# Cross-attention output through DRAM: two rounded parts, or one float32 that the reader splits

## The chip, the cores and the metric

The kernel runs on one core of one Trainium2 chip. The metric is the device time of one execution in microseconds (us), the median of several runs. Five engines work side by side, each through its own queue in a fixed order: PE (matrix products; its weight loads are shown as PEld), ACT, DVE and POOL (elementwise work), and SP, which here issues all DMAs.

## The reference

One step of a hybrid encoder layer on 1024 prompt rows and 8 x 16 sample rows, 1152 token rows in all, in float32. After the three token mixers comes a cross-attention with 4 heads of 256 channels into 256 memory rows, then a gated feed-forward network. What matters here:

```python
def cross_attend(u, mk, mv, wq, wo):
    b, n, _ = u.shape
    q = jnp.einsum('bnd,de->bne', u, wq).reshape(b, n, X_HEADS, X_HEAD_DIM)
    s = jnp.einsum('bnhd,bmhd->bhnm', q, mk.astype(q.dtype)).astype(jnp.float32) * (X_HEAD_DIM ** -0.5)
    pr = jax.nn.softmax(s, axis=-1)
    o = jnp.einsum('bhnm,bmhd->bnhd', pr, mv.astype(jnp.float32)).astype(u.dtype)
    return jnp.einsum('bne,ed->bnd', o.reshape(b, n, D_MODEL), wo)
...
    h = h + mix.astype(h.dtype)
    h = h + cross_attend(rmsnorm(h, p['norm_x_g']), mk, mv, p['wq_x'], p['wo_x']).astype(h.dtype)
    h = h + swiglu(rmsnorm(h, p['norm_ffn_g']), p['w_gate'], p['w_up'], p['w_down']).astype(h.dtype)
```

The tensor `o` of this function, 1024 channels by 1152 token rows, is what the change is about.

## The kernel before

**Products in three parts.** PE multiplies in a rounded 32-bit format (float32r). To keep float32 accuracy, each operand x is split into a high part hi (x rounded, a cast on ACT) and a low part lo (x - hi, a subtraction on DVE or POOL), and a product is three matmuls: hi·hi, hi·lo, lo·hi (`mm3`, L337 to L340). In the profile its three matmuls are thus L338, L339 and L340. `split` (L459, work at L462 on ACT and L463 on DVE) makes the two parts.

**Cross-attention, heads 0 to 2.** `x_query` makes the queries of a head. `x_prompt` takes the 1024 prompt rows in four blocks of 256: `scores` (PE, then `x_softmax`, whose exponentials on ACT are L1484, whose row maxima on DVE are L1478) and `values`, which transposes the weights on PE (L1547), splits them (L1550, L1551) and multiplies them with the memory values into the PSUM bank `pso`. `x_sample` treats the 128 sample rows of the head as one block of 128; its loads of cached keys and values are L1575 and L1599, its products L1609. Each block of a head ends in `x_out`. For heads 0 to 2 it splits the 2 x 128 channels of the block into a high and a low tile and stores both into `o_sc` (named `osc` in the profile), a DRAM tensor with eight slabs of 128 channels and two parts for each. For head 3 (L1514 to L1522) it splits straight from PSUM into the resident tiles `direct`; nothing of head 3 goes through DRAM.

**Buffers.** The tiles `pt` come from a pool of four buffers (L75). The exponentials of the prompt rows, the two parts of the transposed weights and the two output tiles of x_out all use it. An output tile is free again when its store has landed.

**Output projection.** `add_rows` (L1316) multiplies slabs 0 to 3 (heads 0 and 1) with the first half of `wo_x` and adds the result to the residual rows `h` (L1332, on DVE, which frees the PSUM bank). It needs the three chunk tiles `first`, each of 384 token rows and four slabs. `finish_rows` does the same with slabs 4 to 7 and the second half: slabs 4 and 5 (head 2) are loaded into the tiles `direct`, slabs 6 and 7 (head 3) are put there by x_out. `load_chunk` (L1390) loads the high and the low part of a chunk with a DMA each. Another loader, `load_unsplit` (L1395), stood already in the kernel for the mixers' output `mix_sc`: it loads plain float32 into the low half of the tile, casts it into the high half (L1400) and subtracts in place (L1401), two slabs at a time.

**Order.** `loads` (L1688) is woven into head 3's steps: two of its steps behind each step of head 3's prompt rows, while `weave` (L1711) mixes `add_rows` with head 3's sample rows. This is the order in which the program states the work; the final order of each engine's queue is set when the kernel is built, by a planner that follows a simulated timeline (`schedule_with_timeline_sim=True`), with priorities raised for some steps (`hp`). At run time each engine goes through its queue in that order.

Of the kernel before, what the change touches and what calls it, by code (L numbers as in the profile page):

```python
# [8 lines left out]
F32 = mybir.dt.float32  # L9
F32R = mybir.dt.float32r  # L10
# [7 lines left out]
P = 128  # L18
# [6 lines left out]
T = SEQ + DEC_B * DEC_S  # L25
NBLK = T // P
CW = 384
# [30 lines left out]
def f32(x):  # L58
    return x.bitcast(F32)
# [3 lines left out]
def tile_hybrid_step(ctx: ExitStack, tc: tile.TileContext, a: dict):  # L63
    nc = tc.nc
    ACT, DVE, POOL, PE, SP = nc.scalar, nc.vector, nc.gpsimd, nc.tensor, nc.sync
# [38 lines left out]
    def pt_t(dt=F32R):  # L104
        return ptp.tile([P, 512], dt, tag="pt", name="pt")
# [40 lines left out]
    for k0 in (0, 2):  # L146
        first_raw.append(st_t(F32))
        SP.dma_start(out=first_raw[-1].rearrange("p (k n) -> p k n", n=512),
                     in_=a["wk_x"][0][k0 * P:(k0 + 2) * P, 0:512].rearrange("(k p) n -> p k n", p=P))
# [81 lines left out]
    def dram(shape, dt, name):  # L231
        return dr.tile(shape, dt, name=name, tag=name)
# [3 lines left out]
    z_sc = dram([T, 512], F32, "zsc")  # L236
    xbc_sc = dram([D, T], F32, "xbcsc")
    mix_sc = dram([8, P, T], F32, "mixsc")
    o_sc = dram([8, 2, P, T], F32R, "osc")
    fc_sc = dram([4, SEQ], F32, "fcsc")  # L240
    fs_sc = dram([4, DEC_B, PAST], F32, "fssc")
    fn_sc = dram([32, DEC_S], F32, "fnsc")
# [109 lines left out]
    def dense_T(w, uc, jobs, homes=(pd,)):  # L352

        n = 0
        units = [(w_unit([(w, c0, P)], 0, KT), f) for c0, f in jobs]
        for c in range(NCH):
            for (wh, wl), consume in units:
                ps = homes[n % len(homes)]()
                n += 1
                uh, ul = uc[c]  # L360
                for k in range(KT):
                    mm3(ps[:, :CW], wh[:, k, :], wl[:, k, :], uh[:, k, :], ul[:, k, :], k == 0, k == KT - 1)
                later = consume(c, ps[:, :CW])
                flush()
                if later:
                    late.append(later)
                yield
# [91 lines left out]
    def split(hi, lo, src, scale=None):  # L459

        if scale is None:
            ACT.copy(hi, src)  # L462
            DVE.tensor_tensor(out=lo, in0=src, in1=f32(hi), op=ALU.subtract)  # L463
        else:
            ACT.activation(hi, src, AF.Copy, scale=scale)
            DVE.scalar_tensor_tensor(lo, src, scale, f32(hi), ALU.mult, ALU.subtract)

    def consume_qk(i, nb, scale, pk=None, sk=None):
        def consume(c, ps):
            hl = [sg_t(F32R)[:, :CW] for _ in range(2)]  # L470
            split(hl[0], hl[1], ps, scale)
            for x in range(2):
                SP.dma_start(out=f32(qk_sc[i, x, :, c * CW:(c + 1) * CW]), in_=f32(hl[x]))
            if pk is not None:
                kt = pt_t(F32)[:, :CW]
                ACT.copy(kt, ps)

                def rows():
                    tp = pT()
                    for j in range(3):  # L480
                        PE.transpose(tp[:, j * P:(j + 1) * P], kt[:, j * P:(j + 1) * P], ident)
                    kn = sg_t()[:, :CW].rearrange("p (j n) -> p j n", j=3)
                    DVE.tensor_copy(kn, tp[:, :CW].rearrange("p (j n) -> p j n", j=3))
                    nj = 3 if c < 2 else 2
                    SP.dma_start(out=pk[c * CW:c * CW + nj * P, nb * P:(nb + 1) * P]
                                 .rearrange("(j p) n -> p j n", p=P), in_=kn[:, 0:nj])
                    if c == 2:
                        SP.dma_start(out=sk[:, nb * P:(nb + 1) * P], in_=kn[:, 2])
                return rows
        return consume  # L490
# [735 lines left out]
    def chunks(cs):  # L1226
        for c in cs:
            yield from norm_in(c)
            if c == 0:
# [8 lines left out]
    first = dense_T(w_in, uc, [(C_SQ, consume_qk(0, 0, QS)), (C_SQ + P, consume_qk(1, 1, QS)),  # L1238
                               (C_SK, consume_qk(2, 0, None, p_k[0], s_k[0]))],
                    (pd, pd, pS, pS))  # L1240
# [145 lines left out]
    def chunk_t(home=None):  # L1386

        return act_t(home=home).rearrange("p (x k t) -> p x k t", x=2, k=4)

    def load_chunk(t, src, c, k0, nk=4):  # L1390
        for x in range(2):
            SP.dma_start(out=f32(t[:, x, 0:nk]),
                         in_=f32(src[k0:k0 + nk, x, :, c * CW:(c + 1) * CW]).rearrange("k p t -> p k t"))

    def load_unsplit(t, src, c, k0):  # L1395

        SP.dma_start(out=f32(t[:, 1]), in_=src[k0:k0 + 4, :, c * CW:(c + 1) * CW].rearrange("k p t -> p k t"))
        for k in (0, 2):
            hi, lo = (t[:, x, k:k + 2] for x in range(2))
            ACT.copy(hi, f32(lo))  # L1400
            DVE.tensor_tensor(out=lo, in0=f32(lo), in1=f32(hi), op=ALU.subtract)  # L1401
# [15 lines left out]
    for c in range(NCH):  # L1417
        load_unsplit(ch[c], mix_sc, c, 4)
# [92 lines left out]
    direct = []  # L1511

    def x_out(hd, po, c0, n):
        if hd == 3:  # L1514

            for db in range(2):
                for c in range(NCH):
                    b0, b1 = max(c0, c * CW), min(c0 + n, (c + 1) * CW)
                    if b0 < b1:
                        hi, lo = (direct[c][:, x, 2 + db, b0 - c * CW:b1 - c * CW] for x in range(2))  # L1520
                        split(hi, lo, po[db][:, b0 - c0:b1 - c0])
            return  # L1522
        hi, lo = pt_t()[:, :2 * n], pt_t()[:, :2 * n]
        for db in range(2):
            split(hi[:, db * n:(db + 1) * n], lo[:, db * n:(db + 1) * n], po[db])
        for x, src in enumerate((hi, lo)):
            SP.dma_start(out=f32(o_sc[2 * hd:2 * hd + 2, x, :, c0:c0 + n]).rearrange("k p t -> p k t"),
                         in_=f32(src).rearrange("p (k t) -> p k t", k=2))

    def x_prompt(hd, q):  # L1530
        qh, ql, _ = q
# [11 lines left out]
        def values(t, pr):  # L1543
            tp = pT()
            for mb in range(2):
                for i in range(2):
                    PE.transpose(tp[:, mb * 256 + i * P:mb * 256 + (i + 1) * P],  # L1547
                                 pr[:, i * 256 + mb * P:i * 256 + (mb + 1) * P], ident)
            ph, pl = pt_t(), pt_t()
            ACT.copy(ph, tp)  # L1550
            DVE.tensor_tensor(out=pl, in0=tp, in1=f32(ph), op=ALU.subtract)  # L1551
            po = [pO() for _ in range(2)]
            for db in range(2):
                for mb in range(2):
                    sl = slice(mb * 256, (mb + 1) * 256)
                    mm3(po[db], vt[:, 0, mb, db * P:(db + 1) * P],
                        vt[:, 1, mb, db * P:(db + 1) * P], ph[:, sl], pl[:, sl], mb == 0, mb == 1)
            x_out(hd, po, t * 256, 256)
# [29 lines left out]
    def x_sample(hd, q, keys=None):  # L1588
# [51 lines left out]
        for db in range(2):  # L1640
            PE.transpose(tp[:, db * P:(db + 1) * P].rearrange("p (e i t) -> p i e t", e=2, t=DEC_S),
                         on[:, db * P:(db + 1) * P], ident)
        x_out(hd, (tp[:, 0:P], tp[:, P:2 * P]), SEQ, P)
        yield

# [30 lines left out]
    def reload_h(n):  # L1676
        for b in range(len(h), n):
            h.append(st_t(F32) if b < 8 else xc_t()[:, :D])
            SP.dma_start(out=h[b], in_=h_sc[b * P:(b + 1) * P, :])
# [5 lines left out]
    first = [chunk_t(act0) for _ in range(NCH)]  # L1685
    direct.extend(chunk_t(act1) for _ in range(NCH))

    def loads():  # L1688
        for c in range(NCH):
            load_chunk(first[c], o_sc, c, 0)  # L1690
            yield
        for c in range(NCH):
            load_chunk(direct[c], o_sc, c, 4, 2)
            yield
        for b in range(4):
            reload_h(b + 1)
            yield

    smp, ld = x_sample(3, q, keys), loads()
    for _ in range(X0):  # L1700
        next(smp, None)
# [425 lines left out]
```

## Time and profile before

| | |
|---|---|
| runs (3) | 1881.21 us median, 1878.07 to 1885.1 |
| profiled execution | 1885.79 us, of it a span of 1884.1 us from first to last instruction |
| mean granted TensorE clock | 0.984 |
| stores to `osc` | 30, from 852.4 to 988.0 us |
| loads from `osc` | 12, from 963.2 to 999.5 us |
| PE waits ended by `act<-osc` | 2.3 and 0.9 us |
| ACT waits of L1484 ended by `osc<-pt` | 22.8 us in 3, the longest 12.2 |

How to read it: times in the views run from the start of the span. A row of a timeline gives start, duration, engine, line and operation, then written and read tiles ("out<-in"), their size and how many rows it merges; a bracket behind it gives the idle time of the engine just before and whose end released it. A row of the windows gives for each engine its busy time and instruction count in that stretch, then the clock that PE was granted (1.00 is full), the mean busy share of the 16 DMA engines and what they moved. Matmuls are pipelined, so a busy PE is not PE at its peak; SPq rows are DMA issues.

### The profile page before, as it was taken

Reading aid. Unit: us, or ns where it says so; the run is one execution under the profiler, and the core shown is the slowest. Engines: PE = TensorE matmul, PEld = TensorE weight load, DVE = VectorE, ACT = ScalarE, POOL = GpSimd, SP = SyncE. Lnnn points to the kernel's source line nnn. Section 1 sums busy time; section 2 is a strip of 40 time slices with the busy share of each in tenths; the row PEclk is TensorE's granted clock in tenths of the full one; section 3 lists DMA queues with packets and bytes.
Section 4 is the critical chain, followed back from the end, with each engine's and each line's share of the span. In section 5 each row is a group of like instructions: output and inputs, shape, how many; then the busy total and the mean of one; then the engine's idle time right before and its main releaser. Section 6 shows DMA issues by size and latency. Waiting matters only on the chain.

```text
span 1884.1 us, 32106 instructions
## 1 busy us (share of the span) xinstructions
PE 1828.7 (97%) x12008; PEld 1631.7 (87%) x12008; DVE 894.1 (47%) x1798; ACT 794.4 (42%) x1703; POOL 619.6 (33%) x921
## 2 busy tenths in 40 slices
PE   7999989999999999999989989999999999999998
PEld 5899878888967767899978889999999999888886
DVE  3412323576656873455534586333333333455554
ACT  6533543545455762343332474333333333344443
POOL 7622424445115673121012107444444542000000
PEclk9999998999989999999999989999999999999999
DMA  9464754437677883257794124333222223657572
GB/s 336 150 187 152 215 143 126 149 107 211 182 217 252 286 291 102 111 134 184 173 327 156 65 76 110 94 87 78 71 71 71 71 71 93 215 185 243 167 250 90
DMA packets 312028, 296.63 MB, mean 157 GB/s; under 512 B 113340, under 2 KB 263844, under 8 KB 311872
## 3 DMA queue, kind: packets, MB, share of 16 engines
q1 hardware_dynamic: 311872, 294.57, 51.4%
q8 instruction: 95, 1.56, 0.3%
q14 instruction: 61, 0.50, 0.1%
HBM read 225.12 MB, written 69.91 MB: 157 GB/s over the span
## 4 chain that ended last, share of the span: by engine, by line
PE 83%; DMA 7%; DVE 4%; POOL 2%; ACT 2%; SPq 1%; issue 1%; DVEq 0%; POOLq 0%; ACTq 0%
PE psd L1920 11%; PE psd L338 10%; PE psd L339 9%; PE psd L340 9%; PE pst L1920 9%; PE pss L1920 4%; PE pss L338 4%; PE pss L340 4%; PE pss L339 4%; PE pso L1920 2%; PE pst L338 2%; PE pst L339 2%; PE pst L340 2%; PE pso L603 1%; DMA act<-acsc 1%
## 5 line engine op out<-in xcount | busy, mean ns | idle before, releaser
L132 POOL TENSOR_TENSOR wl<-wr,wh 128x256 fp32r<-128x256 f32 (+2 forms) x152 | 117.6, 807 | 245.4 <-ACT wh L292 189.7
L338 PE MATMUL psd<-act,wh 128*128 128x384 f32 x528 | 182.1, 345 | 0.0
L340 PE MATMUL psd<-act,wl 128*128 128x384 f32 x528 | 180.6, 343 | 0.0
L339 PE MATMUL psd<-act,wh 128*128 128x384 f32 x528 | 180.2, 342 | 0.0
L1920 PE MATMUL pst<-bT,tr 128*128 128x256 f32 (+1 forms) x1068 | 155.0, 293 | 0.0
L1920 PEld LDWEIGHTS pst<-bT,tr 128*128 128x128 f32 x1068 | 144.9, 188 | 0.1
L340 PE MATMUL psd<-wh,act 128*128 128x512 f32 (+3 forms) x424 | 137.3, 325 | 0.9 <-DMA act<-osc 0.9
L338 PE MATMUL psd<-wh,act 128*128 128x256 f32 (+3 forms) x414 | 133.8, 327 | 2.8 <-DMA act<-osc 2.3
L339 PE MATMUL psd<-wl,act 128*128 128x256 f32 (+3 forms) x414 | 134.9, 326 | 0.9 <-POOL wl L132 0.9
L1920 PE MATMUL psd<-bT,tr 128*128 128x320 f32 (+1 forms) x912 | 133.1, 295 | 0.2 <-POOL tr L132 0.2
L1920 PEld LDWEIGHTS psd<-bT,tr 128*128 128x128 f32 x912 | 125.1, 189 | 0.4 <-POOL tr L132 0.4
L132 POOL TENSOR_TENSOR tr<-u,tr 128x256 fp32r<-128x256 f32 x110 | 82.5, 780 | 101.4 <-ACT tr L1756 83.6
L253 POOL TENSOR_SCALAR sm<-sm 128x1 f32<-128x1 f32 (+2 forms) x27 | 8.8, 327 | 297.7 <-ACT y L2031 207.6
L1895 DVE TENSOR_TENSOR tr<-tr,pst 128x256 f32<-128x256 f32 (+1 forms) x86 | 38.6, 449 | 139.8 <-ACT tr L1892 106.9
L132 POOL TENSOR_TENSOR ws<-ws 128x256 f32<-128x256 f32 (+2 forms) x100 | 71.3, 741 | 97.8 <-DVE ws L532 84.9
L338 PEld LDWEIGHTS psd<-act,wh 128*128 128x128 f32 x528 | 99.4, 188 | 2.7 <-issue 2.0
L340 PEld LDWEIGHTS psd<-act,wl 128*128 128x128 f32 x528 | 99.2, 188 | 2.6 <-issue 2.3
L339 PEld LDWEIGHTS psd<-act,wh 128*128 128x128 f32 x528 | 99.3, 188 | 1.8 <-issue 1.5
L132 POOL TENSOR_TENSOR tr<-raw,tr 128x256 fp32r<-128x256 f32 x94 | 69.4, 768 | 84.2 <-ACT tr L1756 73.0
L338 PEld LDWEIGHTS psd<-wh,act 128*128 128x128 f32 x414 | 79.8, 193 | 11.0 <-DMA act<-osc 2.5
L1756 ACT CAST tr<-u 128x512 fp32r<-128x512 f32 x130 | 76.6, 620 | 28.7 <-PE pst L1920 5.9
L340 PEld LDWEIGHTS psd<-wh,act 128*128 128x128 f32 x424 | 81.5, 192 | 8.2 <-DMA act<-osc 1.4
(645 smaller groups left out, 4663.2 us busy)
## 6 DMA issues: line engine op xcount, KB each, us to landing
u<-w_down SPq DMA_DIRECT2D x40, 512.0 KB
raw<-w_down SPq DMA_DIRECT2D x26, 512.0 KB
st<-qksc SPq DMA_DIRECT2D x48, 256.0 KB
wr<-w_in SPq DMA_DIRECT2D x44, 256.0 KB
tr<-hidsc SPq DMA_DIRECT2D x55, 192.0 KB
hidsc<-tr SPq DMA_DIRECT2D x34, 288.0 KB
qksc<-sg SPq DMA_DIRECT2D x48, 192.0 KB
wr<-cache_sb_k SPq DMA_DIRECT2D x32, 256.0 KB
```

What stands on the lines that cost most here:

```text
L132: POOL.tensor_tensor(out=out[:, a0:a1], in0=in0[:, a0:a1], in1=in1[:, a0:a1], op=op)
L253: POOL.tensor_scalar(v, ss, inv, EPS, ALU.mult, ALU.add)
L338: PE.matmul(out, ah, bh, start=start, stop=False)
L339: PE.matmul(out, ah, bl, start=False, stop=False)
L340: PE.matmul(out, al, bh, start=False, stop=stop)
L603: return PE.matmul(po[r:r + 64, q_], vt[:, 2 * (k0 + i) + j, :], pfs[i][:, sl], start=start and k0 == 0 and (j == 0 or qp > 0), stop=k0 + ...
L1756: ACT.copy(hi, src)
L1895: DVE.tensor_tensor(out=at(out, g), in0=at(x, g), in1=ps[g][:, :GW[g]], op=op)
L1920: PE.matmul(dst[g][:, :GW[g]], x[:, ka], y[:, k, :], start=start and k == 0 and m == 0, stop=stop and k == 3 and m == 2, skip_group_check= ...
```

## The change

`o_sc` holds one float32 per element in place of two parts. `x_out` copies the two channel halves of a block out of PSUM, one on ACT and one on DVE, into one `pt` tile and stores it with one DMA. Both sets of chunk loads use `load_unsplit`, which now takes the number of slabs; `load_chunk` goes. Head 3's path through `direct` and the arithmetic of the projection stay.

```diff
-    o_sc = dram([8, 2, P, T], F32R, "osc")
+    o_sc = dram([8, P, T], F32, "osc")
...
-    def load_chunk(t, src, c, k0, nk=4):
-        for x in range(2):
-            SP.dma_start(out=f32(t[:, x, 0:nk]),
-                         in_=f32(src[k0:k0 + nk, x, :, c * CW:(c + 1) * CW]).rearrange("k p t -> p k t"))
-
-    def load_unsplit(t, src, c, k0):
-
-        SP.dma_start(out=f32(t[:, 1]), in_=src[k0:k0 + 4, :, c * CW:(c + 1) * CW].rearrange("k p t -> p k t"))
-        for k in (0, 2):
+    def load_unsplit(t, src, c, k0, nk=4):
+
+        SP.dma_start(out=f32(t[:, 1, 0:nk]), in_=src[k0:k0 + nk, :, c * CW:(c + 1) * CW].rearrange("k p t -> p k t"))
+        for k in range(0, nk, 2):
             hi, lo = (t[:, x, k:k + 2] for x in range(2))
             ACT.copy(hi, f32(lo))
             DVE.tensor_tensor(out=lo, in0=f32(lo), in1=f32(hi), op=ALU.subtract)
...
-        hi, lo = pt_t()[:, :2 * n], pt_t()[:, :2 * n]
+        o = pt_t(F32)[:, :2 * n]
         for db in range(2):
-            split(hi[:, db * n:(db + 1) * n], lo[:, db * n:(db + 1) * n], po[db])
-        for x, src in enumerate((hi, lo)):
-            SP.dma_start(out=f32(o_sc[2 * hd:2 * hd + 2, x, :, c0:c0 + n]).rearrange("k p t -> p k t"),
-                         in_=f32(src).rearrange("p (k t) -> p k t", k=2))
+            (DVE.tensor_copy if db else ACT.copy)(o[:, db * n:(db + 1) * n], po[db])
+        SP.dma_start(out=o_sc[2 * hd:2 * hd + 2, :, c0:c0 + n].rearrange("k p t -> p k t"),
+                     in_=o.rearrange("p (k t) -> p k t", k=2))
...
         for c in range(NCH):
-            load_chunk(first[c], o_sc, c, 0)
+            load_unsplit(first[c], o_sc, c, 0)
             yield
         for c in range(NCH):
-            load_chunk(direct[c], o_sc, c, 4, 2)
+            load_unsplit(direct[c], o_sc, c, 4, 2)
             yield
```

## The prediction

> **What bounds the kernel now.** I read the page, then the windows by stage, then the timelines of PE, ACT, DVE and SP around every use of `osc`. The page says that TensorE sets the time:
>
> ```profile
> PE 1828.7 (97%) x12008; PEld 1631.7 (87%) x12008; DVE 894.1 (47%) x1798; ACT 794.4 (42%) x1703; POOL 619.6 (33%) x921
> ```
>
> The windows (busy us of PE, PEld, DVE, ACT, POOL in that order, then the granted clock, DMA share, GB/s) show where the 55 us without a matmul can concern this change:
>
> ```profile
> 852.00:960.00 108.00, 107.53 (x802) 101.19 (x801) 53.68 (x121) 37.17 (x111) 11.59 (x19) 1.00 0.80 192
> 968.00:990.00 22.00, 15.58 (x85) 11.45 (x84) 4.37 (x12) 3.98 (x14) 1.05 (x2) 0.90 1.06 381
> 990.00:1000.00 10.00, 9.53 (x56) 9.29 (x57) 6.33 (x19) 4.96 (x17) 1.79 (x3) 0.71 0.63 200
> 1000.00:1080.00 80.00, 80.00 (x395) 64.92 (x394) 37.38 (x71) 24.39 (x61) 13.68 (x20) 1.00 0.27 97
> ```
>
> The copies and stores of x_out run from 852 us on, and there PE has work for 107.53 of 108 us; whatever they save has nothing to give there. From 1000 us PE is full again. Only between is PE short of work, with the DMA engines full (share 1.06, 381 GB/s) from 968 to 990. The timeline of PE names the gaps (start, duration, what; the bracket is idle time before it and who ended it):
>
> ```profile
> 967.76 0.28 PE L340 MATMUL pso<-pt,vt 128*128 128x256 f32 x1
> 970.38 0.50 PE L338 MATMUL psd<-wh,act 128*128 128x512 f32 x1 [2.34 <-DMA act<-osc]
> ...
> 971.17 0.39 PE L339 MATMUL psd<-wl,act 128*128 128x512 f32 x1
> 972.49 0.80 PE L340 MATMUL psd<-wh,act 128*128 128x512 f32 x1 [0.93 <-DMA act<-osc]
> ...
> 986.19 0.66 PE L1547 MATMUL pst<-ident,pt 128*128 128x128 f32 x4
> 990.01 0.58 PE L338 MATMUL pss<-kt,st 128*128 128x256 f32 x1 [3.17 <-ACT pt L1484]
> ...
> 998.72 0.39 PE L338 MATMUL pso<-pt,vt 128*128 128x256 f32 x1 [0.46 <-DVE act L463]
> ```
>
> The first two gaps (2.34 and 0.93) wait for the high, then for the low part of the first chunk of `osc`. The third (3.17) waits for an exponential of head 3 on ACT, since that frees the PSUM bank of its scores. Behind the second and the third the clock is low:
>
> ```profile
> 972.00:974.00 2.00, 1.51 (x4) 1.22 (x5) 0.00 (x0) 0.00 (x0) 0.00 (x0) 0.50 1.06 373
> 974.00:976.00 2.00, 2.00 (x8) 1.57 (x7) 0.00 (x0) 0.00 (x0) 0.00 (x0) 0.66 1.06 373
> 990.00:992.00 2.00, 1.99 (x9) 1.99 (x10) 0.87 (x4) 0.96 (x2) 1.33 (x3) 0.50 0.54 169
> 992.00:994.00 2.00, 2.00 (x11) 2.00 (x11) 1.58 (x4) 0.04 (x1) 0.47 (x1) 0.50 0.32 101
> 994.00:996.00 2.00, 2.00 (x12) 2.00 (x11) 1.14 (x5) 2.00 (x7) 0.00 (x0) 0.54 1.01 322
> ```
>
> What PE loses by that is its busy time times (1 - clock): 1.51 x 0.50 + 2.00 x 0.34 = 1.44 us, and 1.99 x 0.50 + 2.00 x 0.50 + 2.00 x 0.46 = 2.92 us. With 2.34 + 0.93 + 3.17 and 0.46 ahead of 998.72, **11.3 us** are lost here, the most that the change can win back in this place.
>
> Why was ACT late? Two rows of DVE's timeline, then ACT's:
>
> ```profile
> 965.60 0.68 DVE L1478 TENSOR_REDUCE sm<-pss 128x2 f32<-128x512 f32 x1
> ...
> 986.94 0.29 DVE L463 TENSOR_TENSOR pt<-pst,pt 128x128 fp32r<-128x128 f32 x1 [3.53 <-PE pst L1547]
> ```
>
> ```profile
> 981.54 0.47 ACT L1484 ACTIVATE pt<-pss,sm 128x256 f32<-128x256 f32 x1 [12.22 <-DMA osc<-pt]
> ...
> 983.11 0.27 ACT L462 CAST pt<-pst 128x128 fp32r<-128x128 f32 x1 [0.55 <-DMA osc<-pt]
> 987.26 0.27 ACT L462 CAST pt<-pst 128x128 fp32r<-128x128 f32 x1 [3.89 <-DVE pt L463]
> 988.26 0.62 ACT L292 CAST wh<-wr 128x512 fp32r<-128x512 f32 x1 [0.73 <-DMA wr<-wo_x]
> 988.94 0.47 ACT L1484 ACTIVATE pt<-pss,sm 128x256 f32<-128x256 f32 x1
> ```
>
> The scores of head 3's first two blocks were reduced by 966.3 (965.60 + 0.68), so their exponentials could have run then. But ACT stood 12.22 us because it had no free `pt` buffer (there are four): high and low tiles held them whose stores had not landed. Then x_out of head 2's sample rows needed two more: its first low part (986.94) waited 3.53 us until PE had transposed head 3's weights, the second cast 3.89 us for that, the weight cast 0.73 us for `wo_x`, and only behind these came the exponential at 988.94. The scarce things are thus `pt` buffers and DMA time.
>
> **The change part by part.** Durations first:
>
> ```profile
> L462 ACT CAST pt<-pso 128x256 fp32r<-128x256 f32 x24 | 9.1, 379 | 35.8 <-PE pso L340 32.4 <-DVE pt L463 2.8 <-DMA osc<-pt 0.5
> L463 DVE TENSOR_TENSOR pt<-pso,pt 128x256 fp32r<-128x256 f32 x24 | 10.0, 417 | 16.8 <-ACT pt L462 16.8
> L1629 DVE COPY ws<-pst 128x128 f32<-128x128 f32 x4 | 1.1, 276 | 0.6 <-ACT ws L1629 0.6
> L1400 ACT CAST act<-act x6: 826/832/839, 705.6 to 735.0; 128x768 fp32r<-128x768 f32 x6
> L1401 DVE TENSOR_TENSOR act<-act x6: 948/953/961, 706.4 to 736.6; 128x768 fp32r<-128x768 f32 x6
> ```
>
> x_out: for twelve blocks of prompt rows (24 rows of L462, two a block) one cast (379 ns) and one subtraction (417 ns) go, and of the other two one is a plain copy on ACT and one on DVE, side by side. No row has the 256-wide DVE copy out of PSUM; it lies between the 276 ns of the 128-wide one and the 417 ns of the subtraction; I take 417, and PE's full queue hides either end: **0** on the path. (Without that cover it would be a gain of some 0.4 us a block, since the two copies no longer wait for one another.) One `pt` tile is taken where two were.
>
> Loads and stores (the list of issues, with the KB of each, then SP's queue, which shows when):
>
> ```profile
> osc<-pt SPq DMA_DIRECT2D x24, 256.0 KB
> osc<-pt SPq DMA_DIRECT2D x6, 128.0 KB
> act<-osc SPq DMA_DIRECT2D x6, 768.0 KB
> act<-osc SPq DMA_DIRECT2D x6, 384.0 KB
> ```
>
> ```profile
> 963.17 7.87 SPq L1392 DMA_DIRECT2D act<-osc  x6
> 971.13 1.95 SPq L1527 DMA_DIRECT2D osc<-pt  x1
> ...
> 975.17 0.94 SPq L1392 DMA_DIRECT2D act<-osc  x1
> ...
> 982.47 1.05 SPq L1527 DMA_DIRECT2D osc<-pt  x2
> 984.18 1.73 SPq L324 DMA_DIRECT2D wr<-wo_x  x3
> ```
>
> 30 stores become 15 and 12 loads 6, all of the same size each. SP needed 7.87 us to issue the six large loads, held up by full DMA engines, and the store of head 2's block stood behind them until 971.13. Of the bytes that drop out, three loads of 768 KB, one of 384 KB (the second half of the first direct chunk, 975.17) and two stores of 256 KB (one of the pair begun at 971.13, one of the pair of 982.47) belong to the jam: 3.3 MB, at 381 GB/s **8.6 us** of DMA time. So the `wo_x` loads of 984.18 and the exponentials come about that much sooner, and with one tile a block the exponential of 981.54 needs no landed store at all. What is late next is PE itself: it has its own product rows from 972.49 to 986.85. So I count the third gap and its low clock as gone: **-3.17 - 2.92 = -6.1 us**.
>
> The first gap: one plain load stands where the load of the high part stood, so it lands at 970.38 or up to 0.7 us sooner (256 KB less ahead of it, at 381 GB/s); I take the sooner, and 0.7 us stay for the range. But now ACT (0.832) and DVE (0.953) come behind it, each on two of the four k. The high part is there at 970.5, the low part at 971.5, instead of 970.38 and 972.49. PE's first four products need only the high part and last 1.2 us. So **+0.1** and, the second gap being covered, **-0.9 us**; the low clock of 972 to 976 stays, the 0.46 too.
>
> The splits are new work, 9 casts (7.5 us) and 9 subtractions (8.6 us), on engines that are busy 3.98 and 4.37 of 22 us there. They are still not free: both queues run in a fixed order, and behind a cast that waits for its load stand the exponentials, behind a subtraction the additions L1332 that free PSUM. The nearest row is the same load, of `mixsc`, some 270 us earlier:
>
> ```profile
> 704.61 0.50 PE L338 MATMUL psd<-wh,ws 128*128 128x512 f32 x1 [0.67 <-ACT ws L1382]
> ...
> 708.98 0.66 PE L1178 MATMUL psd<-ident,sg 128*128 128x128 f32 x4 [1.31 <-DVE st L1332]
> ```
>
> There PE lost 1.31 us to an addition that stood behind splits (and 0.67 to a cast). The cost lies between nothing (all splits in idle time) and one gap with its low clock, 6.1; I take the nearest, **+1.3 us**. Sum: -6.1 + 0.1 - 0.9 + 1.3 = **-5.6 us**. The profiled execution took 1885.79 us (span 1884.1 and 1.7 around it), the median of the runs is 1881.21. The stalls should be the same in all, so I take them off the median: **1875.6 us**.
>
> [...]
>
> **The rivals.** *All of it goes* (1). With `pt` buffers free, head 3's exponentials and weights can be ready while the first load travels, and the planner can put their products into the gap at 968. For it: the scores were reduced by 966.3, and ACT stood idle for the 12.22 us ahead of 981.54. Against: the order comes from the planner's own estimate of the loads, which already ran PE into a 2.34 us wait. All 11.3 us: 1870.0 us.
>
> *The stall only moves* (2). The direct chunks still wait for head 2's last store, and a cast for one of them on ACT, ahead of the exponentials, rebuilds the third gap. The wait for `pt` is replaced by a wait for a load: -5.6 + 6.1 = +0.5, 1881.7 us.
>
> *Two such holds: slower* (3). There are two direct chunks that need late stores (columns 384 to 767 and 768 to 1151). If both casts stand ahead of exponentials that PE needs, each costs 6.1 us: -5.6 + 12.2 = +6.6, 1887.8 us. It decides from the point at which ACT is held longer than PE has product rows in its own queue; before, that cover lasted from 972.49 to 986.85. For it: ACT did stand 12.22 us in one wait, with everything behind it. Against: the sample rows of head 2 no longer wait for two `pt` tiles, so those loads start earlier, into emptier DMA engines. [...]
>
> **How the numbers follow.** A difference under 0.5% (9.4 us: below 1871.8 or above 1890.6) can hardly be told from none here. Forecast 0.48, (1) 0.20, (2) 0.17, (3) 0.15. The planner also orders everything anew behind this place, which no row prices; I let it blur each case by some 3 us. Faster: most of (1) and a little of the forecast, 0.20. Slower: (3) blurred upwards, 0.11. Within 0.5%: 0.69. The range reaches from (1) blurred by 1 us to (3): 1869 to 1888; the bounds of the splits' cost (-6.9 with nothing, -0.8 with 6.1) lie within it.
>
> **What would show it.** The page should list 15 stores and 6 loads of `osc`, nine casts of some 0.83 us and nine subtractions of some 0.95 us behind those loads; ACT's wait on `osc<-pt` (12.22 us) gone; the DMA share below 1.0 by 980 us; no PE gap of 3 us ahead of head 3's scores, the clock at 1.00 behind it; a PE gap of about 2.4 us still ahead of the first product row, now ended by ACT. The forecast is wrong if a PE wait ended by a split of a direct chunk, or by an addition L1332, adds up to more than 1.3 us, or if the gaps come back elsewhere behind 1000 us.

## The result: 0.55% faster, and where the time went

| | before | after |
|---|---|---|
| median (6 runs each, taken side by side) | 1882.90 us | 1872.12 us |
| lowest to highest | 1878.07 to 1885.10 us | 1868.48 to 1874.39 us |
| ratio after / before, 95% interval | | 0.9945, 0.993 to 0.996 |
| profiled execution (span) | 1885.79 us (1884.1) | 1873.87 us (1872.2) |
| first exponential of the cross-attention | 836.8 us | 832.5 us |
| first product with tile `bT` in the feed-forward network | 1101.5 us | 1089.2 us |
| **the stretch between these two** | **264.7 us** | **256.7 us** |
| from there to the end of the span | 782.6 us | 783.0 us |

The median lies in the range, 3.5 us below the time forecast, and nearest to rival (1). (The forecast was taken off 1881.21 us, the median of the first three runs; against 1882.90 us the gain is 10.8 us, nearly twice the 5.6 forecast.) In both kernels the products with tile `bT` begin 2.9 us behind the very first product of the feed-forward network, so the stretch measures the same in each. Of the 11.9 us between the two spans, 8.0 lie in the stretch that the change touches. 4.3 lie ahead of it, where both kernels have the same instructions in the same order; that part differs from one profile of a kernel to the next (e12 below). So the stretch is what the experiments are read by.

The page of after, its row for the engines:

```profile
PE 1818.9 (97%) x12008; PEld 1625.1 (87%) x12008; DVE 896.0 (48%) x1792; ACT 796.1 (43%) x1697; POOL 619.1 (33%) x921
```

Against before PE has 9.8 us less busy time (1828.7 before) for the same 12008 matmuls. At a low clock a product counts as busy for longer (in the prediction's rows a 128x512 product has 0.39 us at 971.17 and 0.80 us at 972.49, where the clock is 0.50), so part of the difference shows as busy time and not as idle. The windows of after (length, then busy us of PE, PEld, DVE, ACT, POOL, then granted clock, DMA share, GB/s):

```profile
852.00:960.00 108.00, 106.88 (x811) 100.46 (x810) 54.55 (x121) 36.90 (x109) 9.93 (x16) 1.00 0.77 192
960.00:968.00 8.00, 6.67 (x44) 6.19 (x42) 1.54 (x3) 3.88 (x9) 5.74 (x9) 1.00 0.34 104
968.00:990.00 22.00, 20.76 (x133) 16.62 (x132) 17.32 (x35) 12.77 (x29) 4.19 (x6) 1.00 0.77 279
990.00:1000.00 10.00, 10.00 (x76) 7.66 (x76) 5.70 (x11) 2.98 (x7) 0.00 (x0) 1.00 0.45 134
```

The clock is 1.00 in all of them. In each window the time lost to PE is the idle part plus busy time x (1 - clock). From 960 to 1000 us that is 1.33 + 1.24 + 0 = 2.57 us, where before lost the 11.3 us of the prediction. PE's timeline of after shows what stands behind the last query product:

```profile
963.71 0.34 PE L340 MATMUL psd<-act,wl 128*128 128x384 f32 x1
963.88 1.03 PE L1541 MATMUL pst<-ident,pt 128*128 128x128 f32 x8
965.90 0.39 PE L338 MATMUL pso<-pt,vt 128*128 128x256 f32 x1 [0.99 <-ACT pt L1544]
966.63 0.39 PE L339 MATMUL pso<-pt,vt 128*128 128x256 f32 x1 [0.34 <-DVE pt L1545]
...
967.91 0.28 PE L340 MATMUL pso<-pt,vt 128*128 128x256 f32 x1
969.43 0.50 PE L338 MATMUL psd<-wh,act 128*128 128x512 f32 x1 [1.24 <-ACT act L1395]
...
970.56 1.15 PE L1603 MATMUL pss<-kf,ws 128*32 128x256 f32 x16
971.50 1.12 PE L1603 MATMUL pss<-ws 128*32 128x256 f32 x16
972.55 0.39 PE L338 MATMUL pss<-kt,st 128*128 128x256 f32 x1
```

(Behind the changed lines the numbers are 5 or 6 lower than in before: L1541 transposes weights, was L1547; L1603 was L1609.) The eight transposes and the twelve products into `pso` at 963.88 to 967.91 belong to *head 3*. In before head 3 had only got as far as its first scores here, and the last products into `pso` were still head 2's. Of the idle time, 0.99 and 0.34 us wait for the split of head 3's weights, and 1.24 us wait for the first chunk of `osc`, now for its cast. Behind the first four products of that chunk, head 3's sample rows (L1603) and scores stand where the second gap was. ACT's timeline says why head 3 is ready:

```profile
955.71 0.47 ACT L1479 ACTIVATE pt<-pss,sm 128x256 f32<-128x256 f32 x1 [1.86 <-DVE sm L1474]
...
957.54 0.47 ACT L1479 ACTIVATE pt<-pss,sm 128x256 f32<-128x256 f32 x1
...
968.55 1.57 ACT L1395 CAST act<-act 128x768 fp32r<-128x768 f32 x2 [2.41 <-DMA act<-osc]
```

The exponentials of head 3's first two blocks (L1479, was L1484) run at 955.71 to 958.00, while before the first of them ran at 981.54. Reckoned from the first exponential of the cross-attention, that is 123 against 145 us. The tile `osc` in the trace, its issues and who waited for it:

```profile
L1521 SPq DMA_DIRECT2D osc<-pt x15: 360/413/565, 847.2 to 957.8; - x15
L1392 SPq DMA_DIRECT2D act<-osc x6: 359/468/714, 964.1 to 984.6; - x6
...
  ACT act L1395: 2.9, 3
  DVE pt L1545: 0.7, 1
```

Fifteen stores, the last issued at 957.8 us (before 30, the last at 988.0). ACT's 22.8 us of waiting for stores ahead of exponentials are gone; what waits for a store is one subtraction, for 0.7 us.

### The profile page after: what moved, and what is told of

It is laid out like the page before. It is cut to its first block, busy times and chain, and to the rows that moved or that the text cites. A ratio compares the mean times of both kernels' runs of the same rounds, so it can differ in the third digit from the quotient of the medians.

```text
span 1872.2 us, 32061 instructions
## 1 busy us (share of the span) xinstructions
PE 1818.9 (97%) x12008; PEld 1625.1 (87%) x12008; DVE 896.0 (48%) x1792; ACT 796.1 (43%) x1697; POOL 619.1 (33%) x921
## 4 chain that ended last, share of the span: by engine, by line
PE 82%; DMA 7%; DVE 4%; POOL 3%; ACT 2%; issue 2%; SPq 1%; DVEq 0%; POOLq 0%; ACTq 0%
PE psd L1914 11%; PE psd L338 10%; PE psd L339 10%; PE psd L340 10%; PE pst L1914 8%; PE pss L1914 4%; PE pss L338 4%; PE pss L339 4%; PE pss L340 4%; PE pso L1914 2%; PE pst L338 2%; PE pst L339 2%; PE pst L340 2%; PE pso L603 2%; POOL wl L132 1%
## 5 line engine op out<-in xcount | busy, mean ns | idle before, releaser
L338 PEld LDWEIGHTS psd<-wh,act 128*128 128x128 f32 x414 | 79.9, 193 | 11.1 <-ACT wh L292 1.5
```

Of the source, the lines that this page charges most:

```text
L338: PE.matmul(out, ah, bh, start=start, stop=False)
```

## The experiments

Three explanations stood against each other. **Bytes**: fewer loads and stores in the jam, so all that waits for a DMA comes sooner. **Tiles**: one `pt` tile a block and a shorter hold on it, so head 2 is through sooner and head 3's work is there when PE runs dry. **Chain**: two copies side by side in place of cast and subtraction one behind the other. Against them stands the price of the splits behind the loads. "Before" in the edits is the kernel before, "after" the changed one. The table has, for each profile, the stretch and the time that PE lost in the windows 852 to 1000 us, worked out as above:

| run | median us | ratio to before, 95% | stretch us | lost us | stretch - lost |
|---|---|---|---|---|---|
| before | - | 1 | 264.7 | 11.7 | 253.0 |
| e12, before again | 1882.28 | 0.9995, 0.9982 to 1.0007 | 266.0 | 11.7 | 254.3 |
| after | 1872.12 | 0.9945, 0.993 to 0.996 | 256.7 | 3.7 | 253.0 |
| e11, after again | 1875.08 | 0.9957, 0.9941 to 0.9973 | 255.4 | 2.7 | 252.7 |
| e1, low tile in `sg` | 1908.10 | 1.0128, 1.0107 to 1.0150 | 289.0 | 23.3 | 265.7 |
| e2, two tiles | 1875.82 | 0.9958, 0.9943 to 0.9973 | 258.3 | 6.1 | 252.2 |
| e3, loads twice | 1872.20 | 0.9940, 0.9924 to 0.9956 | 254.5 | 1.8 | 252.7 |
| e4, all bytes twice | 1871.21 | 0.9941, 0.9921 to 0.9960 | 254.6 | 1.9 | 252.7 |
| e5, store side alone | 1872.89 | 0.9947, 0.9927 to 0.9967 | 255.3 | 2.6 | 252.7 |
| e6, load side alone | 1882.71 | 0.9998, 0.9985 to 1.0011 | 268.6 | 15.3 | 253.3 |
| e7, splits twice | 1884.82 | 1.0008, 0.9994 to 1.0021 | 264.4 | 11.1 | 253.3 |
| e8, loads by two slabs | 1878.94 | 0.9969, 0.9952 to 0.9986 | 259.5 | 6.3 | 253.2 |
| e9, chain in one tile | 1873.46 | 0.9953, 0.9934 to 0.9972 | 255.7 | 2.5 | 253.2 |
| e10, addition first | 1874.02 | 0.9950, 0.9935 to 0.9966 | 256.4 | 3.5 | 252.9 |

The last column is the check on the reading: in all but e1 the stretch is 252.2 to 254.3 us plus what PE lost around the hand-over from head 2 to the output projection. Nothing else in these 250 us moves the time. (e1 loses another 12.2 us between 1000 us and the end of the stretch.)

The order of PE's products sorts the profiles in the same way. In after, e11, e2 to e5 and e7 to e10, head 3's first exponential comes 121 to 128 us behind the first of the cross-attention, and 12 products of head 3 into `pso` stand ahead of the first product row. In both profiles of before and in e6 it comes 145 to 148 us behind, and no product of head 3 stands there; e1 has none there either (174 us).

### Both kernels again (e12, e11)

Before and after, unaltered.

> The kernel before, unaltered. What is asked is how far the profiles of one kernel differ from one another, ahead of the cross-attention and in the stretch. Theory (the change works in the stretch alone): the ratio is 1 within its interval; the stretch from the first exponential of the cross-attention to the first gate/up product is 264 to 266 us again, as in the first profile of this kernel (264.7) and unlike the 254.5 to 256.7 of the kernels that gained; the first exponential may stand anywhere from 829 to 837 us, since that part is the same in all kernels. Rival (the later start of 836.8 us belongs to the kernel before): the first exponential stands at 836 to 837 us again.

> The changed kernel again, unaltered, for the comparison beside the others on one chip and for the scatter of the profile: stretch 256 to 258 us, and the first exponential of the cross-attention (836.8 us in the profile before, 832.5 in the one after, all instructions ahead of it being the same in both) at 830 to 837 us if that difference is scatter, at 831 to 834 if it belongs to the kernel. Ratio to before 0.993 to 0.996.

Before again shows three of the four gaps on PE, ended by the same work (the second, 0.93 us for the low part, is not there):

```profile
965.23 0.80 PE L338 MATMUL psd<-wh,act 128*128 128x512 f32 x1 [2.45 <-DMA act<-osc]
...
985.13 0.53 PE L338 MATMUL pss<-kt,st 128*128 128x256 f32 x1 [2.84 <-ACT pt L1484]
...
994.55 0.39 PE L338 MATMUL pso<-pt,vt 128*128 128x256 f32 x1 [0.92 <-DVE act L463]
```

Its stretch is 266.0 us (264.7 in the first profile), that of after again 255.4 (256.7; 256 to 258 was expected). The means differ by 265.35 - 256.05 = 9.3 us, 0.49% of 1882, in keeping with ratios of 0.9945 and 0.9957. The first exponential stood at 831.3 us this time, against 836.8 in the first profile of the same kernel: the 4.3 us ahead of the change are scatter.

### The low part in another pool (e1)

```diff
-        hi, lo = pt_t()[:, :2 * n], pt_t()[:, :2 * n]
+        hi, lo = pt_t()[:, :2 * n], sg_t(F32R)[:, :2 * n]
```

Before with one `pt` tile a block instead of two; bytes and chain stay.

> The stretch is measured from the first exponential of the cross-attention to the first gate/up product: 264.6 us in the profile before (836.8 to 1101.4), 256.6 after (832.5 to 1089.1). The kernel before, all bytes kept (two parts stored and loaded), but x_out takes its low tile from the sg pool, so that it needs one pt tile, as after. Tile theory (the gain comes from the pt tiles): the stretch falls to 256 to 259 us, total ratio to before 0.995 to 0.997. Byte theory (the gain comes from the DMA time saved): 263 to 266 us, ratio 0.998 to 1.001.

It is slower by 1.28%, which neither theory had expected. The `sg` pool has four tiles too, and the memory of the next head and the sample rows need them. PE's timeline:

```profile
961.37 0.74 PE L1503 MATMUL pst<-ident,sg 128*128 128x128 f32 x4 [1.44 <-DMA sg<-mksc]
...
986.62 0.66 PE L1627 MATMUL pst<-ident,sg 128*128 128x128 f32 x2 [4.35 <-DVE sg L1488]
...
1005.17 1.10 PE L1503 MATMUL pst<-ident,sg 128*128 128x128 f32 x4 [5.29 <-DMA sg<-mksc]
```

PE waits for a load into an `sg` tile and for an operation of the sample rows on one, up to 5.29 us at a time. So the run does not speak on the `pt` tiles: it gave one scarce pool relief at the cost of another. That the `sg` tiles were short because they waited for their stores fits these waits, but no row shows it directly.

### Two tiles, copies side by side (e2)

```diff
-        o = pt_t(F32)[:, :2 * n]
+        o = [pt_t(F32)[:, :n] for _ in range(2)]
         for db in range(2):
-            (DVE.tensor_copy if db else ACT.copy)(o[:, db * n:(db + 1) * n], po[db])
-        SP.dma_start(out=o_sc[2 * hd:2 * hd + 2, :, c0:c0 + n].rearrange("k p t -> p k t"),
-                     in_=o.rearrange("p (k t) -> p k t", k=2))
+            (DVE.tensor_copy if db else ACT.copy)(o[db], po[db])
+        for db in range(2):
+            SP.dma_start(out=o_sc[2 * hd + db, :, c0:c0 + n], in_=o[db])
```

After with two `pt` tiles a block again.

> The changed kernel, all bytes as after, but x_out takes two pt tiles again, one for each channel half, each with a store of half the size. Tile theory: the exponentials of head 3 wait for landed stores again, the stretch goes back to 262 to 266 us, ratio to before 0.998 to 1.001. Byte theory: it stays at 256 to 259 us, ratio 0.994 to 0.997.

Most of the gain stays (0.9958), with 6.1 us lost against 2.7 and 3.7. Head 3's transposes and products still stand ahead of the first product row, but its weights come later:

```profile
965.30 0.38 PE L338 MATMUL pso<-pt,vt 128*128 128x256 f32 x1 [2.66 <-ACT pt L1544]
```

Behind that gap of 2.66 us the clock is low (0.85 in the window 960 to 968, 0.90 in 968 to 990). So the second tile is worth some 3 us here, not the whole. The 258.3 us lie where the byte theory had put this run and not where the tile theory had (262 to 266): taken alone, e2 speaks against the tiles, and e4 and e5 below had to decide.

### The bytes (e3, e4)

e3 loads every chunk twice from `osc` (into the high half, then into the low half, from which the splits work as in after). e4 also stores x_out's tile into a second DRAM tensor, and the extra load comes from that, so that all bytes and DMAs of before are back:

```diff
-    def load_unsplit(t, src, c, k0, nk=4):
+    def load_unsplit(t, src, c, k0, nk=4, twin=None):
...
+        if twin is not None:
+            SP.dma_start(out=f32(t[:, 0, 0:nk]), in_=twin[k0:k0 + nk, :, c * CW:(c + 1) * CW].rearrange("k p t -> p k t"))
...
+        SP.dma_start(out=o2_sc[2 * hd:2 * hd + 2, :, c0:c0 + n].rearrange("k p t -> p k t"),
+                     in_=o.rearrange("p (k t) -> p k t", k=2))
```

> The changed kernel with each chunk of the attention output loaded twice (first also into the half of the tile that the cast then overwrites), so that the loads move as many bytes as before; stores and tiles as after. Byte theory: the chunks land about 6 us later in all, the stretch goes back to 261 to 265 us. Tile theory: 257 to 259 us, since only the first product row waits some 2 us longer.

> As the kernel with doubled loads, and x_out's one tile is stored twice as well, to two DRAM tensors, of which the second feeds the doubled load: all bytes as before, one pt tile per block as after. Byte theory: the stretch is 263 to 266 us, ratio to before 0.998 to 1.001. Tile theory: 257 to 260 us, ratio 0.995 to 0.998.

Both keep all of the gain (0.9940 and 0.9941), with stretches some 2.5 us under what even the tile theory expected. e4's windows and PE's waits there:

```profile
968.00:990.00 22.00, 22.00 (x154) 17.82 (x146) 17.16 (x35) 13.20 (x30) 3.94 (x4) 1.00 1.05 383
```

```profile
963.76 0.38 PE L339 MATMUL pso<-pt,vt 128*128 128x256 f32 x1 [1.00 <-ACT pt L1549]
...
964.49 0.38 PE L340 MATMUL pso<-pt,vt 128*128 128x256 f32 x1 [0.34 <-DVE pt L1550]
...
966.31 1.22 PE L1608 MATMUL pss<-kf,ws 128*32 128x256 f32 x16 [0.26 <-POOL ws L1591]
```

The DMA engines are as full as in before (1.05, 383 GB/s, against 1.06 and 381), and PE has no gap at all from 968 to 990: head 3's work (L1608 and the scores behind it) stands where PE waited for the first chunk. The byte theory falls, for one tile a block and copies side by side.

### One side alone (e5, e6)

e5 is before with x_out's side of the change: one tile, two copies, stored twice, into both parts. Loads, DRAM tensor and bytes are those of before; **it leaves out the splitting**. e6 is before with the load side's work: behind each load the nine casts and nine DVE operations of the same size, which leave the values as they are.

```diff
-        hi, lo = pt_t()[:, :2 * n], pt_t()[:, :2 * n]
+        o = pt_t(F32)[:, :2 * n]
         for db in range(2):
-            split(hi[:, db * n:(db + 1) * n], lo[:, db * n:(db + 1) * n], po[db])
-        for x, src in enumerate((hi, lo)):
+            (DVE.tensor_copy if db else ACT.copy)(o[:, db * n:(db + 1) * n], po[db])
+        for x in range(2):
...
-                         in_=f32(src).rearrange("p (k t) -> p k t", k=2))
+                         in_=o.rearrange("p (k t) -> p k t", k=2))
```

```diff
+        for k in range(0, nk, 2):
+            hi, lo = (t[:, x, k:k + 2] for x in range(2))
+            ACT.copy(hi, f32(hi))
+            DVE.tensor_tensor(out=lo, in0=f32(lo), in1=f32(lo), op=ALU.max)
```

> Both parts of the change apart. The store side alone: x_out copies into one tile as after and stores that tile twice, into the two places of the high and the low part; the chunk loads are those of before, with no split behind them, so the splitting of this tensor is left out. All bytes as before. If the store side (one tile, copies side by side, hence another order of the queues) makes the gain: stretch 254 to 259 us (before 264.7, after 256.7), ratio to before 0.993 to 0.997. If the load side makes it: 262 to 266 us, ratio 0.998 to 1.001.

> The load side alone: x_out of before (two tiles, two stores), both parts loaded as before, and behind each load a cast of the high part onto itself on ACT and a pass of the low part through DVE (the larger of it and itself), so that nine casts and nine DVE operations of the size of the splits stand there. If the store side makes the gain: stretch 264 to 270 us, ratio 1.000 to 1.003. If it is the splits behind the loads that make the planner put head 3's work ahead of the first product row: 255 to 259 us, ratio 0.994 to 0.997.

The store side alone makes the whole gain (0.9947, stretch 255.3); the load side alone none (0.9998, stretch 268.6). e5 waits for its first chunk, e6 for the operations behind it and again for head 3's exponential (L1488 there):

```profile
965.31 0.47 PE L338 MATMUL psd<-wh,act 128*128 128x512 f32 x1 [1.04 <-DMA act<-osc]
```

```profile
972.24 0.50 PE L338 MATMUL psd<-wh,act 128*128 128x512 f32 x1 [2.99 <-ACT act L1396]
...
974.57 0.80 PE L340 MATMUL psd<-wh,act 128*128 128x512 f32 x1 [1.15 <-DVE act L1397]
...
993.10 0.39 PE L338 MATMUL pss<-kt,st 128*128 128x256 f32 x1 [2.73 <-ACT pt L1488]
```

e5's 1.04 us ended by the load stands where after has 1.24 us ended by the cast, so in after the splits cost about 0.2 us net (0.3 by the 1.38 us of e11).

### Chain or tile (e9)

```diff
-            (DVE.tensor_copy if db else ACT.copy)(o[:, db * n:(db + 1) * n], po[db])
+            part = o[:, db * n:(db + 1) * n]
+            ACT.copy(part, po[db])
+            DVE.tensor_tensor(out=part, in0=po[db], in1=part, op=ALU.max)
```

After with four operations a block one behind the other, as in before's split, but in one tile.

> What on the store side makes the gain: one tile in place of two, or two copies side by side in place of four operations one behind the other. The changed kernel with one tile and one store, but for each channel half a copy on ACT and behind it a DVE operation on the same data (the larger of the PSUM value and the copy, the same number), so that x_out has its four operations and their chain again. If the four operations in a chain are what held head 2 back: stretch 261 to 266 us, ratio to before 0.997 to 1.001. If it is the number of tiles: 254 to 258 us, ratio 0.993 to 0.997. (Two tiles with the copies side by side had 258.3 us.)

The gain stays (0.9953, stretch 255.7). One tile without the short chain suffices, then, and two tiles with the short chain (e2) nearly do; before has two tiles and the long chain. But both runs also have half the bytes of before. With all bytes, apart from e1, only one tile and the short chain together were run (e4, e5), so it is not shown that either would do alone with before's bytes. The trace of e9 holds a surprise as to *how*:

```profile
  ACT pt L1521: 17.1, 3
```

ACT still waits 17.1 us for stores of `osc`, now ahead of x_out's own copy. But that no longer costs PE anything, since head 3's transposes and products stand ahead of the first product row all the same. So ACT's wait as such was not the price; what had to wait behind it was.

### The price of the splits (e7, e8, e10)

e7 does the splits of the `osc` loads (and of the others that use this loader) twice over; e8 loads two slabs at a time, so that a split waits for half a load; e10 raises the priority of the addition L1332 that frees PSUM.

```diff
             ACT.copy(hi, f32(lo))
             DVE.tensor_tensor(out=lo, in0=f32(lo), in1=f32(hi), op=ALU.subtract)
+            ACT.copy(hi, f32(lo))
...
+            DVE.tensor_tensor(out=lo, in0=f32(lo), in1=f32(hi), op=ALU.add)
+            DVE.tensor_tensor(out=lo, in0=f32(lo), in1=f32(hi), op=ALU.subtract)
```

```diff
-        SP.dma_start(out=f32(t[:, 1, 0:nk]), in_=src[k0:k0 + nk, :, c * CW:(c + 1) * CW].rearrange("k p t -> p k t"))
         for k in range(0, nk, 2):
             hi, lo = (t[:, x, k:k + 2] for x in range(2))
+            SP.dma_start(out=f32(lo), in_=src[k0 + k:k0 + k + 2, :, c * CW:(c + 1) * CW].rearrange("k p t -> p k t"))
```

```diff
-                    DVE.tensor_tensor(out=h[blk][:, sl], in0=h[blk][:, sl], in1=ps.pop(blk), op=ALU.add)
+                    with tc.high_priority(100):
+                        DVE.tensor_tensor(out=h[blk][:, sl], in0=h[blk][:, sl], in1=ps.pop(blk), op=ALU.add)
```

> The price of the splits: the changed kernel with each cast done twice and each subtraction done three times (subtract, add back, subtract), 9 more casts and 18 more DVE operations. If the splits cost what was put down for them (1.3 us for one set, on additions that wait behind them), this is 2 to 5 us slower than the changed kernel, stretch 259 to 262 us. If they lie in idle time: 256 to 258 us.

> The changed kernel with each chunk load cut in two, two slabs (384 KB) each, so that the first cast can start when half of the first chunk has landed. The gap ahead of the first product row (1.24 us in the profile after) should fall to 0 to 0.4 us, the stretch to 255 to 256.5 us; ratio to before 0.993 to 0.996, not told apart from the changed kernel. If the gap is set by something else than the landing of the load, it stays above 1 us.

> The changed kernel with a raised priority for the residual addition L1332, as the second projection half already has for its own, so that the planner puts it ahead of the splits on DVE. In the changed kernel no PE wait behind splits is left after 970 us, so by that the time should stay (stretch 255 to 257 us, ratio to the changed kernel 0.999 to 1.001); also in the earlier use of the same function the 1.3 us wait of a PE product for this addition (at 708.98 us before) should go, 1 us less ahead of the cross-attention.

e7 gives the whole gain back (1.0008, stretch 264.4; neither expectation went so far), though head 3's work still fills the hand-over. At the loads of `mixsc`, which use the same loader, next to nothing of this shows: PE waits 1.88 us there, against 0.42 + 1.33 us in after. e7's windows and PE's two waits:

```profile
968.00:990.00 22.00, 14.80 (x62) 11.87 (x62) 21.69 (x31) 13.45 (x24) 6.20 (x4) 0.84 0.66 239
```

```profile
973.95 0.50 PE L340 MATMUL psd<-wh,act 128*128 128x512 f32 x1 [3.60 <-DVE act L1399]
...
985.56 0.80 PE L338 MATMUL psd<-wh,act 128*128 128x512 f32 x1 [3.60 <-DVE st L1332]
```

DVE is busy 21.69 of 22 us; PE waits 3.60 us for a low part and 3.60 us for an addition queued behind low parts, and the clock falls to a mean of 0.84. e8 gets rid of the wait ahead of the first product row and finds another, for an addition behind splits:

```profile
981.27 0.66 PE L338 MATMUL psd<-wh,act 128*128 128x512 f32 x1 [2.77 <-DVE st L1332]
```

2.77 us, with a mean clock of 0.92 in that window: the stretch is 259.5 us where 255 to 256.5 was expected (by the medians it cannot be told from after, the intervals overlap). e10 has the time of after, but it tells nothing on the price: the additions stand between the same splits on DVE as in after, and the wait in the earlier use that was to go is still there (1.34 us, in after 1.33). So the splits cost almost nothing as the change has them, with DVE busy 17.32 of 22 us, but there is no room for more.

## Why the prediction came out as it did

**The bound held.** 11.3 us were named as the most that could be won. PE lost 11.7 us in the windows 852 to 1000 of both profiles of before, and the stretch follows that loss one for one through 13 profiles.

**The third gap and its low clock (-6.1)** went, with the size forecast; the clock is 1.00 through 1000 us. Of the two reasons given, the `pt` tile is borne out (e5, e9) and the 8.6 us of DMA time fall: e4 has all the bytes and the full gain. The way was another, too. The forecast left head 3's exponentials behind the first gap and let them come about 8.6 us sooner, while PE did product rows; they come some 22 us sooner and stand ahead of that gap. One reading was wrong here: by 966.3 only the first block's scores had been reduced. The second block's reduction (L1478) ran at 979.34, behind two additions L1332 that waited for PE, so in that order its exponentials could not have run before.

**The first two gaps: here the step failed.** The prediction let PE run dry at 968 as before, with a gap of 2.34 + 0.1 us, and kept the low clock behind it (1.44) and the 0.46 us. It held the order of PE's work as given, though it named the way out as rival (1): head 3's weights ready, its products put into the gap. That is what happened. By terms: 11.3 - 5.6 = 5.7 us should have remained, of it 2.44 for the first gap, 0.03 for the second, 1.44 and 0.46 that stay, and 1.3 for the splits. 2.57 us remained: 0.99 + 0.34 for head 3's weights and 1.24 for the first chunk, and no low clock. The difference is 3.1 us. By the stretch the gain was 8.0 us in the first pair of profiles and 9.3 by the means of both pairs, where the forecast had 5.6. Rival (1) erred the other way: it took all 11.3 us, and 2.57 stayed. That the median fell into the range was thus partly luck: the range reached down to rival (1), and it was rival (1)'s mechanism that came.

Why was it given 0.20 only? The argument against it was that the planner had already run PE into a 2.34 us wait, so its estimate of the load must be off. As I read the traces now, the planner had nothing else to put there in before: a shortage of tiles is part of its plan, not only of the run. Up to about 845 us the queues of both kernels have the same order; from there on PE's order differs, with head 2's work sooner. That this order, and not the waits of the run, makes the gain is read from the orders and timelines; no run held the order fixed and gave back the tile, so it is not shown by experiment. How much of the relief is the tile and how much the shorter chain is not settled either: with half the bytes each keeps most of the gain without the other (e9, e2).

**The copies (0).** The 256-wide DVE copy out of PSUM was taken at 417 ns, the other nine casts at 0.83 and subtractions at 0.95 us. The groups of lines of after, 830 to 1000 us:

```profile
L1396 DVE TENSOR_TENSOR act<-act 128x768 fp32r<-128x768 f32 x9 | 8.9, 1015 | 2.9 <-ACT act L1395 2.8
...
L1395 ACT CAST act<-act 128x768 fp32r<-128x768 f32 x9 | 7.1, 837 | 2.9 <-DMA act<-osc 2.9
L1520 DVE COPY pt<-pso 128x256 f32<-128x256 f32 x12 | 5.0, 418 | 10.5 <-ACT pt L1520 10.5
```

418, 837 and 1015 ns. That they cost and gain nothing on PE's path by themselves is right as far as e9 shows it (four operations: 255.7, two: 256.7 and 255.4).

**The splits (+1.3).** The mechanism is real (e7, e8), its size here is 0.2 to 0.3 us net, reckoned from one profile of e5 and two of after. The row from which the price was taken, an addition held behind splits, did not recur behind 960 us; a cast took the place of the load in a gap that is there without splits too (e5).

**The rivals (2) and (3)** did not come: no exponential stood behind a cast that waited for a direct chunk, and head 2's last store left 6 us ahead of the first load (957.8, 964.1). What (3) describes does happen when the splits are doubled, with two waits of 3.60 us and a time back at before's.

**The marks named beforehand** were all there but the last: the page lists 15 stores and 6 loads, the share of the DMA engines is 0.77 from 968 to 990 (0.41 from 976 to 980), and the gap ahead of the first product row, now ended by ACT, is 1.24 us and not 2.4.

**The planner's order behind this place** was to blur the time by some 3 us. From the first product with tile `bT` to the end, all fourteen profiles have 782.3 to 784.4 us.

## What to carry to other kernels

When a queue stands still for a buffer, look not only at what the stall costs but at what other work the freed buffer lets the planner put into the gaps next to it: here the first two gaps with the low clock behind them gave back 2.6 of the 8.7 us that PE won between 960 and 1000 us, where the forecast had them cost half a us more. A second tile that must wait for its store was dear in this pool of four (e2: 6.1 us lost, against 3.7 and 2.7 in after), and a pool that looks free next to it may be just as short (e1: PE waits of up to 5.29 us). Full DMA engines say nothing by themselves (e4: a share of 1.05, with PE busy 22.00 of 22.00 us): ask which wait of PE a transfer ends, and give the bytes back in an experiment before crediting the gain to them.

## What the hardware showed beside that

**Full DMA engines need not cost PE anything.** In e4 the DMA share was 1.05 at 383 GB/s for 22 us while PE was busy 22.00 of 22.00 us at full clock.

**Behind a gap of 1.5 us the clock was at 0.50 for 17 us, behind two of 2.7 us for less than half as long.** Before's first profile, PE's timeline and then the windows around it:

```profile
547.50 0.43 PE L943 MATMUL pso<-pt,act 128*32 128x128 f32 x8 [1.49 <-ACT act L935]
```

```profile
545.00:550.00 5.00, 3.47 (x73) 2.94 (x76) 3.67 (x13) 2.97 (x7) 0.00 (x0) 0.87 0.08 22
550.00:555.00 5.00, 5.00 (x26) 3.48 (x18) 2.57 (x8) 0.50 (x2) 0.00 (x0) 0.50 0.63 212
...
560.00:565.00 5.00, 5.00 (x20) 3.68 (x18) 1.77 (x7) 2.13 (x4) 0.00 (x0) 0.50 0.84 208
565.00:570.00 5.00, 5.00 (x30) 2.37 (x30) 3.10 (x11) 2.56 (x5) 0.00 (x0) 0.93 0.88 267
```

PE was idle for 1.49 us; then it was busy without a break, at 0.50 until past 565 us. In before again the same product waited 0.25 us and the clock stayed at 1.00 in the windows from 545 to 565 us. Behind the waits of 2.66 (e2) and 2.77 us (e8) it was low for some 7 and 3 us (windows of 1 us each), while the waits of 0.99, 0.34 and 1.24 us in after brought no low clock. So in these profiles the length of a gap does not tell how long the clock is low behind it. Why it stayed low for 17 us in before, with PE busy all through, is open; how much of the 5.5 us by which the two profiles of before differ at their first exponential is due to that stretch was not measured.
